# All eight row groups of the up pairs in a 7-product form, more low parts by accumulating DMA, and new order tables

## The chip, the cores and the metric

The kernel runs on one core of a Trainium2 chip. The metric is the device time of one execution in microseconds: the median of the runs that were taken. Lower is better.

## The reference

One inference step of a hybrid diffusion backbone with one trunk layer, for 128 context tokens and 128 latent tokens (both request groups use the same weights, so 256 rows go through every weight matrix):

```python
D_MODEL = 2048; D_FF = 4 * D_MODEL; IN_WIDTH = 8704
sh1, sc1, g1, sh2, sc2, g2 = ada_mod(c_ctx, w_ada, b_ada)       # SiLU(c) @ w_ada + b_ada
h = rms_norm(xp, norm1_w) * (1 + sc1) + sh1
qa, ka, va, qb, kb, vb, ga, gb = project_heads(h, w_in, ...)
oa = context_attention(qa, ka, va, sink)                        # latent: window / neighbourhood attention
ob = context_attention(qb, kb, vb, None)
xp = xp + g1 * merge_branches(oa, ob, ga, gb, w_br_a, w_br_b, w_out)
h2 = rms_norm(xp, norm2_w) * (1 + sc2) + sh2
xp = xp + g2 * sq_relu_mlp(h2, w_up, w_down)                    # relu(h2 @ w_up) ** 2 @ w_down
```

All is float32. The outputs are both groups' tokens and the new keys and values.

## The kernel before

**Products.** Each float32 operand is split in a high part (a rounded copy, by ScalarE) and a low part (the operand less its high part), and a product is three matmuls: high by high, high by low, low by high. A matmul takes a 128x128 stationary operand (128 rows of the contracted dimension, 128 tokens) and 512 moving columns of a weight.

**Steps.** The weights stream through in 456 steps, one 128x1024 float32 tile (0.524 MB) each. `add_step` records a step, `run` (L284 on) emits all of them in one order for all engines, ahead of the run; nothing is scheduled by the machine except that each engine and queue runs its own list in order and waits on semaphores. Per step the raw tile is loaded on SP's queue, ScalarE makes `wH` (`prep_hi`), VectorE makes `wL` (`prep_b`), TensorE multiplies. Steps 0 to 71 are the first input projections, 72 to 135 the gates, 136 to 167 the branches, 168 to 199 `w_out`, 200 to 215 up units 0 and 1. Then come seven periods of 32 steps: an up pair p (units 2p and 2p+1 of 512 columns of `w_up`, 16 steps) and the four down units of pair p-1 (4 steps each); at last four down units (440 to 455).

**Tables that set the order.** `RUN[i]` says how many steps ahead of step i raw tiles are requested, `LOOK[i]` how many steps ahead high and low parts are made; high parts go one step further (`HI_AHEAD`). `LO_DMA` lists the steps whose low part is made by DMA: ScalarE writes the negated high part (`minus_plus`, L265), then a DMA issued by GpSimd (POOL's queue) adds the raw weight to it from HBM (L266). `DOTS`, `DOTS2`, `POST`, `JOBS` and others place side work (dot products for the modulation, attention, transposes of activations) at steps.

**Buffers.** Nearly all tiles come from one pool, `G`, of GEN = 50 general buffers of 4 KB per partition. A load waits until the buffer it takes is free.

**Up pairs.** In `up_pair` a row group is 256 rows of the contracted dimension: two halves k, two token groups s and the two units n make a 2x2 by 2x2 block product, 8 products. Six of the eight row groups (0, 2, 3, 5, 6, 7) are done with 7 products on sums of blocks, into seven PSUM banks Q1 to Q7: the weights come rearranged (`in_w_upF`) as tiles X and Y, `y_sums` and `y_split` make the sums t and u with their high and low parts on VectorE and ScalarE, and `fast_stat` prepares the sums of the stationary side once (`sH`, `sL`, for three of the four groups of h2). Row groups 1 and 4 are plain: two weight tiles, 8 products, some of them into an eighth bank Z, which VectorE adds at the end. After a pair, `up_act` (relu, square), `up_planes`, `up_flip` (a DMA transpose on SP's queue), `up_T` and `up_T_lo` turn its output into stationary operands `aH`, `aL` for the down units.

**Down units.** Down unit n of piece p adds to a running sum of 512 output columns; for n = 1, 2, 3 the sum is copied out of PSUM, stored to HBM by POOL (`sm`), loaded back on SP (`sum_back`) and seeded into PSUM by ScalarE. Gates in `AWAY` are stored and loaded back in the same way.

## Time and profile before

| what | value |
|---|---|
| runs | 1316.84, 1318.39, 1317.2 us; median 1317.2 |
| span of the profiled execution | 1317.5 us |
| its mean granted TensorE clock | 0.998 |
| one period (up pair and four down units) | 83.0 us |
| low parts by accumulating DMA | 33 (21 of them in the seven periods) |
| DMA, whole span | 417.98 MB, mean 317 GB/s |

The profiled execution's own time is its span, 1317.5 us, since what lies around it is not part of the page; it stands 0.3 us from the median. The page lists busy time by engine, where PE is TensorE's matmul, PEld its weight load, DVE VectorE, ACT ScalarE, POOL GpSimd and SP SyncE. A busy share is a mean over stages with different limits, so the stages are looked at one by one.

### The profile page before, as it was taken

The numbers are of one execution on the slowest core, as the hardware profiler recorded it, in microseconds if no ns is written. First come the engines' busy times: TensorE is split into PE (matmuls) and PEld (weight loads), VectorE is DVE, ScalarE is ACT, GpSimd is POOL, SyncE is SP. The second block draws the span as 40 slices with busy tenths as digits, with TensorE's granted clock in tenths as the row PEclk, the third lists the DMA queues.
The fourth block names the chain that finished last, engine by engine and source line by source line (L and its number), as shares of the span: only waits on it lengthen the run. The fifth ranks groups of instructions, "written<-read, shape, count | busy, mean of one in ns | idle before, by whom it ended". The sixth has DMA issues, their size and how long they took to land.

```text
span 1317.5 us, 18232 instructions
## 1 busy us (share of the span) xinstructions
PE 1304.1 (99%) x6320; PEld 1061.0 (81%) x6320; DVE 1149.2 (87%) x1490; ACT 915.0 (69%) x1282; POOL 78.3 (6%) x99
## 2 busy tenths in 40 slices
PE   8999999999999999999999999999999999999998
PEld 4777788788888878888888888888888888888876
DVE  4478899985999989999899799897988988979996
ACT  5534766788766555654788868969779688796772
POOL 0000003211000000000000000100101001010010
PEclk9999999999999999999999999999999999999999
DMA  9999999987699999997489878989989799899994
GB/s 371 408 408 409 408 335 358 370 304 285 210 367 340 371 371 330 340 388 267 163 264 324 271 256 292 291 295 296 323 293 291 265 313 305 286 287 370 351 345 168
DMA packets 154972, 417.98 MB, mean 317 GB/s; under 512 B 52688, under 2 KB 53952, under 8 KB 154880
## 3 DMA queue, kind: packets, MB, share of 16 engines
q1 hardware_dynamic: 146128, 386.54, 79.9%
q0 software_dynamic: 8560, 30.18, 9.9%
q8 instruction: 49, 0.80, 0.3%
q14 instruction: 43, 0.35, 0.1%
q10 hardware_dynamic: 192, 0.10, 0.1%
HBM read 389.19 MB, written 17.61 MB: 309 GB/s over the span
## 4 chain that ended last, share of the span: by engine, by line
PE 97%; DMA 2%; ACT 0%; DVE 0%; issue 0%
PE acc L312 17%; PE acc L314 17%; PE acc L313 17%; PE Q L1211 7%; PE Q L1213 7%; PE Q L1212 6%; PE acc L423 5%; PE acc L424 5%; PE acc L425 5%; DMA araw<-in_w_pair 2%; PE ps_ada L329 2%; PE ps_S L775 1%; PE acc L1028 1%; PE acc L1046 1%; PE acc L1029 1%; PE acc L1044 1%
## 5 line engine op out<-in xcount | busy, mean ns | idle before, releaser
L101 ACT ACTIVATE wH<-raw 128x1024 fp32r<-128x1024 f32 (+1 forms) x375 | 378.3, 1045 | 122.8 <-DMA raw<-in_w_in 19.7
L259 DVE TENSOR_TENSOR wL<-raw,wH 128x1024 fp32r<-128x1024 f32 x336 | 399.7, 1223 | 50.8 <-ACT wH L101 28.1
L423 PE MATMUL acc<-wH,hH 128*128 128x512 f32 x276 | 108.8, 394 | 0.0
L425 PE MATMUL acc<-wH,hL 128*128 128x512 f32 x276 | 107.6, 390 | 0.0
L424 PE MATMUL acc<-wL,hH 128*128 128x512 f32 x276 | 107.6, 390 | 0.0
L312 PE MATMUL acc<-wH,hH 128*128 128x512 f32 x256 | 102.4, 400 | 0.0
L314 PE MATMUL acc<-wH,hL 128*128 128x512 f32 x256 | 99.9, 390 | 0.0
L313 PE MATMUL acc<-wL,hH 128*128 128x512 f32 x256 | 99.8, 390 | 0.0
L1422 DVE CUSTOM_DVE_ANT_0 aT<-aT,cB,cols 128x1024 f32<-128x1024 f32 x60 | 76.4, 1289 | 0.1
L1422 DVE CUSTOM_DVE_ANT_0 junk<-aT,cB,cols 128x1024 bf16<-128x1024 f32 x60 | 76.4, 1290 | 0.0
L423 PEld LDWEIGHTS acc<-wH,hH 128*128 128x128 f32 x276 | 51.8, 188 | 12.9 <-issue 2.1
L101 ACT ACTIVATE uH<-raw 128x1024 fp32r<-128x1024 f32 x42 | 44.4, 1057 | 24.0 <-DVE raw L1270 22.9
L425 PEld LDWEIGHTS acc<-wH,hL 128*128 128x128 f32 x276 | 51.8, 188 | 11.0
L424 PEld LDWEIGHTS acc<-wL,hH 128*128 128x128 f32 x276 | 51.9, 188 | 10.3
L1276 DVE TENSOR_TENSOR tL<-t,tH 128x1024 fp32r<-128x1024 f32 x42 | 51.3, 1221 | 8.6 <-ACT tH L101 8.6
L101 ACT ACTIVATE tH<-t 128x1024 fp32r<-128x1024 f32 x42 | 44.3, 1056 | 20.6 <-DVE t L1266 15.0
L312 PEld LDWEIGHTS acc<-wH,hH 128*128 128x128 f32 x256 | 48.1, 188 | 10.1 <-issue 0.7
L314 PEld LDWEIGHTS acc<-wH,hL 128*128 128x128 f32 x256 | 48.1, 188 | 10.2
L313 PEld LDWEIGHTS acc<-wL,hH 128*128 128x128 f32 x256 | 48.2, 188 | 9.8 <-issue 0.5
L1266 DVE TENSOR_TENSOR t<-raw 128x1024 f32<-128x1024 f32 x42 | 51.2, 1220 | 1.8 <-PE acc L314 1.4
L1258 DVE TENSOR_TENSOR XL<-raw,XH 128x1024 fp32r<-128x1024 f32 x42 | 51.2, 1220 | 0.4 <-DMA sm<-dsum 0.4
L1276 DVE TENSOR_TENSOR uL<-raw,uH 128x1024 fp32r<-128x1024 f32 x42 | 51.2, 1219 | 0.0
(626 smaller groups left out, 3387.8 us busy)
## 6 DMA issues: line engine op xcount, KB each, us to landing
raw<-in_w_in SPq DMA_DIRECT2D x133, 512.0 KB, 9.4
raw<-in_w_down SPq DMA_DIRECT2D x128, 512.0 KB, 6.5
raw<-in_w_upF SPq DMA_DIRECT2D x84, 512.0 KB, 5.6
araw<-in_w_pair SPq DMA_DIRECT2D x72, 512.0 KB, 10.2
aT<-in_w_gT SPq DMA_DIRECT2D x64, 512.0 KB, 8.5
aT<-in_w_adaT SPq DMA_DIRECT2D x56, 512.0 KB, 9.0
raw<-in_w_up SPq DMA_DIRECT2D x44, 512.0 KB, 6.3
raw<-in_w_out SPq DMA_DIRECT2D x32, 512.0 KB, 10.4
```

The costliest lines, as they stand in the source:

```text
L101: act.activation(out, in_, AF.Copy)
L259: dve.tensor_tensor(st["lo"], st["raw"], st["hi"].bitcast(F32), op=OP.subtract)
L312: pe.matmul(acc[tb], sh, wh[:, k, :], start=f, stop=False, **kw)
L313: pe.matmul(acc[tb], sh, wl[:, k, :], start=False, stop=False, **kw)
L314: pe.matmul(acc[tb], sl, wh[:, k, :], start=False, stop=l, **kw)
L423: pe.matmul(acc[tb], sh, wh[:, k, :], start=kt == 0 and k == 0 and not held and not seeded, stop=False, **kw)
L424: pe.matmul(acc[tb], sh, wl[:, k, :], start=False, stop=False, **kw)
L425: pe.matmul(acc[tb], sl, wh[:, k, :], start=False, stop=last and k == 1 and not hold, **kw)
L1211: pe.matmul(acc, stat[0], hi, start=f, stop=False)
L1213: pe.matmul(acc, stat[1], hi, start=False, stop=l)
L1276: dve.tensor_tensor(b[n + "L"], v, b[n + "H"].bitcast(F32), op=OP.subtract)
L1422: dve.tensor_tensor_reduce(out, box["raw"], cB[s, tag], 1.0, dst if second else baT[:, part, fb:fb + 1], OP.mult, OP.add, dst)
```

## The change

Row groups 1 and 4 of the seven pairs take the 7-product form too. The stationary sums of the fourth group of h2 (`fast_stat(3)`) find no buffers of their own: they are written over halves of `h2H`/`h2L` that only up units 0 and 1 read, after up unit 1. Bank Z and its additions fall away. `LO_DMA` grows from 33 to 86 steps and may now hold X tiles (`x_lo_dma`); the low parts of `a2` and `a3` come the same way (`TL_DMA`). Where X's low part is still made by VectorE, it moves into `y_sums` (`XLO_IN`). Four of the running sums stay in their buffers (`STAY`), four gates instead of five go away and back. GEN is 54: the descriptor scratch of GpSimd's DMAs shrinks to 2048, a small pool of scratch tiles is replaced by general buffers. Joins of transposed halves, relu, square and the copies around them are placed one by one (`U_AT`), the lead of high parts has a table of its own (`HIA`), and all order tables are new. The new functions `qk_planes`, `qk_flip`, `qk_join` and `probs_planes` are not called, since `POST` and `JOBS` give three and five places.

```diff
-GEN = 50
+GEN = 54
-FAST = {1: (0, 2, 3, 5, 6, 7), ...}
+FAST = {1: (0, 1, 2, 3, 4, 5, 6, 7), ...}
-AWAY = [('gB', 2), ('gA', 0), ('gB', 0), ('gA', 2), ('gB', 3)]
+AWAY = [('gB', 0), ('gB', 3), ('gA', 1), ('gB', 1)]
-HI_AHEAD = 1
+HIA = "000012322005501123521100232312000100221230331146547320002112220001012200000001..."
-LO_DMA = [57, 92, 106, 114, 116, 127, 165, 172, 184, 196, 224, 232, 237, 256, ...]
+LO_DMA = [45, 47, 51, 67, 83, 84, 85, 91, 92, 94, 98, 100, 110, 112, 116, 118, ...]
+XLO_IN = True
+STAY = [(3, 1), (3, 2), (5, 2), (5, 3)]
+TL_DMA = [2, 3]
...
 def lo_dma(st):
+    if "lo_dma" in st:
+        st.pop("lo_dma")(st)
+        return
...
+            def x_lo_dma(st, b=b):
+                if "prep_a" in st:
+                    st.pop("prep_a")()
+                b["XL"] = G("XL", F32R)
+                minus_plus(b["XL"], b["XH"], st["src"])
...
+        if g == 3:
+            for q in range(nfast - 6):
+                for i in range(2):
+                    dst = [x[2 * q + i].rearrange("p (c k) s t -> p c k s t", k=2)[:, :, 0, 1, :] for x in (h2H, h2L)]
+                    split(*dst, t[:, 2 * i:2 * i + 2, q, :])
+            return
...
         def sc(j, c):
+            if j > 5:
+                g, k = 2 * (j - 6) + c // 2, 2 * (c % 2)
+                return h2H[g][:, k, 1, :], h2L[g][:, k, 1, :]
             return sH[j // 2][:, c, j % 2, :], sL[j // 2][:, c, j % 2, :]
...
-        if seeded and p < last:
+        if seeded and p < last and (p - 1, n) not in STAY:
             load_at(len(wsteps) - SUM_BACK, lambda: sum_back(p, n))
...
-            if n in SEED_N and p < last - 1:
+            if n in SEED_N and p < last - 1 and (p, n) not in STAY:
...
+            for n, places in zip(PIECES[p + 1], U_AT[p]):
+                fs = (lambda n=n: up_act(n, AF.Relu), lambda n=n: up_act(n, AF.Square), lambda n=n: up_planes(n, (0,)),
+                      lambda n=n: up_planes(n, (1,)), lambda n=n: up_flip(n), lambda n=n: join_half(("a", n), 0),
+                      lambda n=n: join_half(("a", n), 1), lambda n=n: up_hi(n), lambda n=n: up_T_lo(n))
...
-    nc = bacc.Bacc("TRN2", target_bir_lowering=False, num_devices=1)
+    nc = bacc.Bacc("TRN2", target_bir_lowering=False, num_devices=1, dynamic_dma_scratch_size=2048)
```

What this does to TensorE's list, in pair 1. Before, the first six matmuls of plain row group 1, whose first tile goes into Q2 and Q4 (two such sets of six per tile, two tiles):

```order
L1211 MATMUL Q2_6518<-wH_6371,h23H_6028 128x512
L1212 MATMUL Q2_6518<-wL_6401,h23H_6028 128x512
L1213 MATMUL Q2_6518<-wH_6371,h23L_6029 128x512
L1211 MATMUL Q4_6535<-wH_6371,h23H_6028 128x512
L1212 MATMUL Q4_6535<-wL_6401,h23H_6028 128x512
L1213 MATMUL Q4_6535<-wH_6371,h23L_6029 128x512
```

Now every row group has products of X, YB, t and u; these are the first twelve matmuls of the seventh, with stationary sums out of `h20H` and `h21H`:

```order
L1295 MATMUL Q1_6535<-XH_6709,h23H_6064 128x512
L1296 MATMUL Q1_6535<-XL_6725,h23H_6064 128x512
L1297 MATMUL Q1_6535<-XH_6709,h23L_6065 128x512
L1295 MATMUL Q3_6579<-XH_6709,h21H_6034 128x512
L1296 MATMUL Q3_6579<-XL_6725,h21H_6034 128x512
L1297 MATMUL Q3_6579<-XH_6709,h21L_6035 128x512
L1295 MATMUL Q2_6537<-YB_6729,h23H_6064 128x512
L1296 MATMUL Q2_6537<-YB_6729,h23H_6064 128x512
L1297 MATMUL Q2_6537<-YB_6729,h23L_6065 128x512
L1295 MATMUL Q5_6581<-tH_6796,h20H_6023 128x512
L1296 MATMUL Q5_6581<-tL_6797,h20H_6023 128x512
L1297 MATMUL Q5_6581<-tH_6796,h20L_6024 128x512
```

The 24 matmuls of a plain row group have become 21; over the program TensorE's list is 42 matmuls of 128x512 shorter.

VectorE's list before, at the start of pair 2: the first row group (t13 and the halves of raw are the sums, XL, tL, uL low parts), then the two low parts of plain row group 1:

```order
L1266 TENSOR_TENSOR t13_7102<-raw_6983,raw_7002 128x1024
L1268 TENSOR_TENSOR raw_7002<-t13_7102,raw_6983 128x512
L1269 TENSOR_TENSOR YB_7103<-raw_7002,YB_7103 128x512
L1270 TENSOR_TENSOR raw_7002<-raw_7002 128x512
L1258 TENSOR_TENSOR XL_7109<-raw_6983,XH_7078 128x1024
L1276 TENSOR_TENSOR tL_7128<-t13_7102,tH_7127 128x1024
L1276 TENSOR_TENSOR uL_7132<-raw_7002,uH_7131 128x1024
L259 TENSOR_TENSOR wL_7158<-raw_7055,wH_7125 128x1024
L259 TENSOR_TENSOR wL_7176<-raw_7057,wH_7156 128x1024
```

The same place now:

```order
L1361 TENSOR_TENSOR t13_7100<-raw_7060,raw_7062 128x1024
L1363 TENSOR_TENSOR YB_7101<-raw_7062,YB_7101 128x512
L1364 TENSOR_TENSOR raw_7062<-t13_7100,raw_7060 128x512
L1367 TENSOR_TENSOR raw_7062<-raw_7062 128x512
L1361 TENSOR_TENSOR t13_7198<-raw_7064,raw_7082 128x1024
L1363 TENSOR_TENSOR YB_7199<-raw_7082,YB_7199 128x512
L1364 TENSOR_TENSOR raw_7082<-t13_7198,raw_7064 128x512
L1367 TENSOR_TENSOR raw_7082<-raw_7082 128x512
L1373 TENSOR_TENSOR tL_7206<-t13_7100,tH_7205 128x1024
L1373 TENSOR_TENSOR uL_7210<-raw_7062,uH_7209 128x1024
```

XL has left for the DMA queue here, the second row group has its own sums in place of two low parts, and its sums stand ahead of the first one's splits.

GpSimd's list before, from pair 1 to pair 2 (`sm` are sums stored away):

```order
L266 DMA wL_6504<-in_w_up 128x1024
L266 DMA wL_6726<-in_w_down 128x1024
L266 DMA wL_6844<-in_w_down 128x1024
L1353 DMA sm01_7053<-dsum1_7050 128x1024
L1353 DMA sm02_7152<-dsum2_7149 128x1024
L1353 DMA sm03_7216<-dsum3_7213 128x1024
```

And now, the last transfers of pair 1, its down units and the start of pair 2:

```order
L272 DMA XL_6725<-in_w_upF 128x1024
L272 DMA XL_6774<-in_w_upF 128x1024
L272 DMA wL_6987<-in_w_down 128x1024
L272 DMA XL_7086<-in_w_upF 128x1024
L272 DMA XL_7097<-in_w_upF 128x1024
L1452 DMA sm01_7126<-dsum1_7123 128x1024
L1452 DMA sm02_7196<-dsum2_7193 128x1024
L272 DMA XL_7248<-in_w_upF 128x1024
L1452 DMA sm03_7283<-dsum3_7280 128x1024
L272 DMA XL_7285<-in_w_upF 128x1024
```

All eight low parts of X in pair 1 come by this queue; the sums now stand between accumulating transfers. Over the program POOL issues 88 of those instead of 33, 50 of them in the seven periods.

204 lines of the change are left out of this document (135 added, 69 removed).

## The prediction

> **What bounds the kernel now.** I read the page first: its busy table and the chain that ended last.
>
> ```profile
> span 1317.5 us, 18232 instructions
> PE 1304.1 (99%) x6320; PEld 1061.0 (81%) x6320; DVE 1149.2 (87%) x1490; ACT 915.0 (69%) x1282; POOL 78.3 (6%) x99
> PE 97%; DMA 2%; ACT 0%; DVE 0%; issue 0%
> ```
>
> TensorE has work in 99% of the span, and 97% of the chain is its own work: at almost every step the instruction before it on PE is what held it. But a matmul's end is modelled, so I looked next at the table by stage. I cut it at the first matmul of each stage; 683.3 is the start of up pair 1, and each later row up to 1181.3 is one period (an up pair, then the four down units of the pair before). Columns: length, then busy time and count of PE, PEld, DVE, ACT and POOL, granted clock, DMA share, GB/s.
>
> ```profile
> 456.60:548.00 91.40, 91.40 (x454) 74.45 (x453) 85.41 (x115) 56.03 (x55) 1.72 (x2) 1.00 1.01 347
> 683.30:766.20 82.90, 82.90 (x367) 68.70 (x366) 71.62 (x81) 67.91 (x72) 3.74 (x5) 1.00 0.87 279
> 766.20:849.20 83.00, 83.00 (x368) 68.73 (x367) 76.37 (x86) 66.20 (x73) 4.25 (x6) 1.00 0.86 287
> 849.20:932.10 82.90, 82.90 (x367) 68.70 (x366) 73.52 (x82) 65.95 (x73) 4.26 (x6) 1.00 0.91 287
> 932.10:1015.10 83.00, 83.00 (x367) 68.74 (x367) 73.83 (x82) 66.62 (x74) 5.13 (x7) 1.00 0.91 306
> 1015.10:1098.10 83.00, 83.00 (x368) 68.75 (x367) 72.54 (x82) 64.98 (x72) 4.30 (x6) 1.00 0.88 291
> 1098.10:1181.30 83.20, 83.20 (x369) 68.77 (x368) 75.53 (x84) 66.59 (x76) 5.35 (x8) 1.00 0.91 303
> 1181.30:1267.00 85.70, 83.37 (x367) 68.38 (x366) 81.64 (x98) 63.30 (x70) 4.53 (x7) 1.00 1.01 353
> 1267.00:1317.50 50.50, 45.60 (x194) 37.13 (x194) 40.23 (x58) 18.16 (x24) 5.04 (x8) 0.94 0.66 227
> ```
>
> By the program a period holds 174 matmuls of an up pair (58 products of three) and 192 of the down units, all of 128x512, so 366 in 83.0 us: **0.2268 us each**, at the full granted clock (1.00), the same in every period. The periods have no PE idle time at all, so each matmul taken out there is time taken out. The one place where PE waits late in the program is the end of the seventh period (83.37 of 85.70). The chain in order of time (start, us, what) shows it:
>
> ```profile
> 1264.49 1.06 ACT dsum L101 x2
> 1265.61 0.78 issue
> 1266.38 0.61 ACT acc L101
> ```
>
> There PE waits some 2.7 us for banks that ACT first has to empty and seed.
>
> **What is removed.** A plain row group costs 2 weight tiles x 2 k x 2 token groups = 8 products, the 7-product form 7. Two row groups in seven pairs change, each product being three matmuls: 2 x 7 x 3 = 42 matmuls x 0.2268 = **-9.5 us**, all on the path. The stationary operands stay as many per product, so the rate should not change. From the profile's own 1317.5 (the runs' median is 1317.2, so the two agree within 0.3) this gives 1308.0.
>
> **What it adds to VectorE and ScalarE.**
>
> ```profile
> L259 DVE TENSOR_TENSOR wL<-raw,wH 128x1024 fp32r<-128x1024 f32 x336 | 399.7, 1223 | 50.8 <-ACT wH L101 28.1 <-PE acc L313 9.4 <-issue 8.1
> L1276 DVE TENSOR_TENSOR tL<-t,tH 128x1024 fp32r<-128x1024 f32 x42 | 51.3, 1221 | 8.6 <-ACT tH L101 8.6
> L1266 DVE TENSOR_TENSOR t<-raw 128x1024 f32<-128x1024 f32 x42 | 51.2, 1220 | 1.8 <-PE acc L314 1.4 <-PE acc L313 0.5
> L1258 DVE TENSOR_TENSOR XL<-raw,XH 128x1024 fp32r<-128x1024 f32 x42 | 51.2, 1220 | 0.4 <-DMA sm<-dsum 0.4
> L1268 DVE TENSOR_TENSOR raw<-t,raw 128x512 f32<-128x512 f32 x42 | 29.1, 692 | 1.4
> L1269 DVE TENSOR_TENSOR YB<-raw,YB 128x512 fp32r<-128x512 f32 x42 | 28.8, 685 | 2.0 <-ACT YB L101 2.0
> L1311 DVE TENSOR_TENSOR up<-up,Z 128x512 f32<-128x512 f32 x7 | 4.8, 688 | 0.2
> L1422 DVE CUSTOM_DVE_ANT_0 aT<-aT,cB,gc_g 128x1024 f32<-128x1024 f32 x32 | 40.6, 1282 | 0.1
> L101 ACT ACTIVATE tH<-t 128x1024 fp32r<-128x1024 f32 x42 | 44.3, 1056 | 20.6 <-DVE t L1266 15.0 <-PE Q L1213 2.1 <-PE Z L1213 1.6
> L101 ACT ACTIVATE XH<-raw 128x1024 fp32r<-128x1024 f32 x42 | 44.2, 1052 | 8.5 <-PE Q L1212 4.6 <-DMA raw<-in_w_upF 2.2 <-PE Q L1213 1.2
> L265 ACT ACTIVATE wL<-wH 128x1024 fp32r<-128x1024 f32 x33 | 35.1, 1063 | 1.1
> L101 ACT ACTIVATE YB<-raw 128x512 fp32r<-128x512 f32 x42 | 25.9, 618 | 3.7 <-PE Z L1213 2.8 <-PE acc L313 0.8 <-PE Q L1212 0.2
> ```
>
> A row group in the new form costs DVE t, tL, uL, XL (4 x 1.22), two sums of half width (2 x 0.692) and YB (0.685): 6.95 us. The plain one cost two low parts, 2.45. For 14 groups: +63.0; the seven additions of Z go, -4.8. Against this stand the low parts taken off DVE. In the stretch of the seven periods 21 of them came by DMA, and now 50 do (48 of weights, two of activations): 29 x 1.22 = -35.4. In all **DVE +22.8 us** there. Its busy time there is the sum of the seven rows, 525.1 of 583.7; now it is 548 of the 574.2 that PE needs, 95% where it was 90%. ACT gets XH, YB, tH, uH for two wH (3.78 for 2.1), 14 times, +23.5, and 29 negated copies of 1.063, +30.8: 461.6 becomes 516, 90%. Both engines still fit below PE; that is the cover, and with 26 us of DVE room over seven periods it is thin. If it were gone, each further us on DVE would be a us of span.
>
> Over the rest of the program 26 more low parts leave DVE (26 x 1.22 = 32 us) and come to ACT and the DMA queues; DVE gains room there, and I cost it at nothing.
>
> **The last stretch.** In the seventh period DVE had 81.64 busy of 85.70, since dot products for the last gate stand there. There the two groups add 13.9 to DVE, plain low parts by DVE (two) go, -2.45, two more low parts come by DMA, -2.4, Z goes, -0.7, and two dot jobs of two 1.28 us each move out to the next unit, -5.1: +3.2, so 84.8 of work for 84.3 us (85.7 less 1.36). I take **+2 us** for it, between -2.7 (the wait at 1264 vanishes) and +5 (the dots gain nothing by moving).
>
> **What it adds to the DMA engines.**
>
> ```profile
> q1 hardware_dynamic: 4481, 16.32, 102.3%
> ...
> q0 software_dynamic: 215, 0.82, 105.4%
> ...
> q0 software_dynamic: 713, 2.62, 54.2%
> q1 hardware_dynamic: 1021, 3.71, 47.6%
> ...
> q1 hardware_dynamic: 146128, 386.54, 79.9%
> q0 software_dynamic: 8560, 30.18, 9.9%
> ...
> pTa<-pla SPq DMA_TRANSPOSE x16, 5.2
> ```
>
> The first row is a stretch of 40 us (100 to 140) with plain loads alone, full at a share of 102%: 0.524 MB in 40 x 0.524 / 16.32 = 1.284 us. The second is 4 us (1091 to 1095) with only POOL's queue, full as well: 4 x 0.524 / 0.82 = **2.56 us for one accumulating transfer**, two loads' worth. From the whole page it comes dearer: q0's 9.9% are 130.4 us for 57.6 units of 0.524 MB, of which 33 accumulate; the others at q1's mean (79.9% for 738 units, 1.43 us) leave 95.2 / 33 = 2.9 us. So 2.56 to 2.9.
>
> Is there room? I count the stretch of seven periods by the order of the queues: 224 weight loads, 36 sums out and back, 29 loads for dots, 12 for conditions and x1, at 1.284 = 387; 15 transposes at 3.2 (my estimate, half way between one load and the 5.2 us to landing), 48; 21 accumulating at 2.56, 54: 489 of 583.7. Afterwards there are 29 more, and eight sum transfers fewer: 489 + 74 - 10 = 553 of 574. The third and fourth rows (843 to 863, full at 102%) test such a count: 3.71 MB of q1, three accumulating transfers and two sums of q0 make 9.1 + 7.7 + 2.6 = 19.4 of 20 us, 3% short. With this 3% the engines need 570 of 574: **nearly a tie with PE**. At 2.9 it is 588, and PE would run dry. I take 2.56, the row in which the queue was alone, and cost the tie at nothing: at 456.60 the engines stood at 1.01 for 91 us and PE did not wait.
>
> ```profile
> HBM read 389.19 MB, written 17.61 MB: 309 GB/s over the span
> ```
>
> The Trainium skill (Perfetto Trace Analysis, Identifying the Most-Contended Engine) would judge this otherwise: DMA by the use of HBM's bandwidth, not by occupancy, which 16 engines make misleading. By that rule 309 GB/s, against the 409 that 16.32 MB in 40 us are, leave a quarter free, and the DMA rival below falls away. This trace differs: from 843 to 863 the engines are full while (2.62 + 3.71) / 20 us is 317 GB/s, because accumulating transfers cost twice their bytes. I keep the rival.
>
> **Smaller edits, each nothing.** XL is computed among y's sums instead of ahead of them, on the same engine. `fast_stat` of group 3 waits for the end of up unit 1, whose matmuls read the halves it overwrites; queued behind its copies on ACT are pair 1's first XH. Its data are wanted 12 steps on, 28 us later; if ACT's lead is lost, a us or two. Split joins, relu and square in pieces, and scratch in general buffers change who waits in the shadow of PE. STAY and one gate fewer spare ten transfers. More prepared in POOL's queue means sums queue behind low parts there, and POOL is busy 6%.
>
> **Rivals.**
> 1. *The DMA engines become the bound*, in the seven periods. At 2.9 us the excess is 588 - 574 = 14 us: 1308 + 14 = **1322** (1315 to 1330), slower. It decides from about 2.64 us per accumulating transfer on, where the count passes 574. For it: the tie, and seven periods without a slack one. Against: a stretch at 1.01 with no PE wait. The Trainium skill (Trainium Kernel Development and Optimization, Key Constraints) has the ground of it: transfers of SP, ACT and POOL share the same 16 DMA engines, so a second queue brings no second bandwidth.
> 2. *VectorE becomes the bound*, at the up pairs, where all of t, u and YB are needed. In the second one it has no room even now, and lives on what it prepared before:
>
> ```profile
> 766.20:805.70 39.50, 39.50 (x176) 32.70 (x175) 39.12 (x43) 26.01 (x29) 1.42 (x2) 1.00 0.82 284
> ```
>
> If a period loses 1 us to it, seven take back 7: **1315**, the same as before. For: 95% over the stretch. Against: the period from 1181 ran at 95% (81.64) and lost 2.3.
> 3. *PE runs without any wait*: 1308.0 - 2.7 = **1305**. That needs the end wait gone, though DVE there gets fuller.
>
> That the change would not do what it says can be set aside: the order on PE has the 42 matmuls fewer.
>
> **How the numbers follow.** Forecast: 1308.0 + 2 = **1310**, own range 1306 to 1314, chance 0.63. Rival 1: 0.17, rival 2: 0.14, rival 3: 0.06. Faster by over 0.2% (which is about what a measurement of this kernel can tell from no change) means below 1314.6, slower above 1319.8: faster 0.63 + 0.06 + 0.05 of rival 2 = 0.74; the rest of rival 2 and a little of rival 1, 0.11, are the same; slower 0.15. The range 1305 to 1321 leaves out most of rival 1 and the lower half of rival 3.
>
> **What would show it.** Right: a period of 81.6 us with PE busy throughout, DMA share about 1.0, DVE about 77 and ACT about 74 of it, and a wait of a few us around the last period's end. Rival 1: PE or ACT waiting for `raw`, `wL` or `XL` transfers at a share of 1.02. Rival 2: PE waiting for `tL`, `uL` or `wL` of DVE with the DMA share below 1. What would make it wrong most easily is the order: prepared less far ahead in many places, a late low part meets PE at once.

## The result, and the profile after

The changed kernel takes **1347.66 us** (median of 4 runs, 1345.13 to 1353.53) against 1317.02 us for before (1316.61 to 1318.39): ratio 1.0233, interval 1.021 to 1.0257. It is 30 us slower, where 1310 was forecast, and outside the range given. The profiled execution has a span of 1345.3 us; its run took 1347.07, so what lies around a span is some 1.8 us. It is 1.8 us for before too (in the runs beside e1 a time of 1316.76 us has a span of 1315.0). So the profiled execution of before, span 1317.5, was a run of some 1319.3 us by this estimate, 2 us above its median and not 0.3, and the forecast took a span for a time. All comparisons by stage below are of span with span.

First the page of the changed kernel: its span, the busy table, and the chain that ended last by engine.

```profile
span 1345.3 us, 18444 instructions
PE 1306.6 (97%) x6278; PEld 1055.0 (78%) x6278; DVE 1142.5 (85%) x1506; ACT 984.1 (73%) x1388; POOL 125.0 (9%) x150
PE 60%; DMA 21%; issue 9%; DVE 6%; ACT 2%; POOL 0%; SPq 0%; ACTq 0%; DVEq 0%; POOLq 0%
```

The 42 matmuls are gone (6278 for 6320), and VectorE is busy 7 us less than before. But the chain, 97% TensorE's own before, is now 60% that and 21% DMA. The table by stage (same columns as in the prediction; `...` stands for a row left out; from 688.10 on each row is one period; the last row is the four down units of the last pair and the end, called the last unit below):

```profile
455.70:548.20 92.50, 92.09 (x454) 74.32 (x453) 84.00 (x113) 53.50 (x55) 1.73 (x2) 1.00 1.05 361
548.20:628.30 80.10, 77.79 (x345) 63.66 (x344) 74.64 (x99) 48.12 (x57) 6.78 (x8) 1.00 1.01 359
...
688.10:785.30 97.20, 86.68 (x362) 70.64 (x361) 74.29 (x90) 72.37 (x85) 8.10 (x10) 0.95 1.03 268
785.30:871.00 85.70, 82.17 (x361) 67.40 (x360) 78.41 (x90) 73.83 (x85) 7.76 (x10) 1.00 0.99 315
871.00:954.00 83.00, 82.34 (x362) 67.36 (x362) 77.38 (x88) 69.88 (x81) 7.77 (x10) 1.00 0.97 314
954.00:1036.80 82.80, 82.36 (x362) 67.32 (x360) 75.21 (x86) 69.84 (x82) 6.63 (x8) 1.00 0.94 299
1036.80:1118.90 82.10, 81.93 (x362) 67.53 (x361) 75.51 (x86) 71.15 (x82) 9.52 (x12) 1.00 1.01 311
1118.90:1210.00 91.10, 85.48 (x363) 68.83 (x362) 79.78 (x90) 75.65 (x89) 6.55 (x9) 0.96 0.90 286
1210.00:1291.90 81.90, 81.90 (x361) 67.45 (x361) 78.72 (x96) 66.28 (x76) 5.75 (x8) 1.00 1.01 343
1291.90:1345.30 53.40, 44.87 (x195) 35.64 (x193) 40.81 (x57) 22.23 (x28) 6.87 (x10) 1.00 0.81 273
```

A period without waits should take 360 matmuls at 0.2268 us, 81.6 us. The fifth and the seventh do. The loss is lumped: **15.6 us in the first period, 9.5 in the sixth, 4.1 in the second**, and outside the periods some 3 us each in the output stage (80.1 us; 77.05 before) and in the last unit (53.4; 50.5 before). The seven periods together take 603.8 us, 29.6 more than the prediction's 574.2.

The first period's loss lies in its up pair (53.65 us; the rest of the period takes the 43.5 us of 192 matmuls). The waits of 700 to 736 us (us in total, times, longest), and the one piece of the chain there that is not TensorE's:

```profile
DVE uL L1373 <- DMA pTa<-pla: 11.9, 1, 11.9
PE Q L1296 <- DMA XL<-in_w_upF: 5.3, 1, 5.3
PE Q L1296 <- DVE uL L1373: 5.2, 1, 5.2
```
```profile
701.17 31.68 DMA pTa<-pla
```

So TensorE waits twice in it: 5.3 us for a low part of X that comes by accumulating transfer (issued at 702.45, landed 15.1 us later; the median of these is 8.7), and 5.2 us for a low part of u, before which VectorE stood 11.9 us until a DMA transpose had landed. That low part does not read what the transpose writes; by the code, both take their buffers from the pool `G`, and it waits for one that the transpose still holds. The transpose, of up unit 1's output, took **31.7 us to land**; before, the median was 5.2. The timeline of SP's queue and that of POOL's (start, length of the issue) show what it met:

```profile
701.17 14.23 SPq L953 DMA_TRANSPOSE pTa<-pla  x1
715.49 7.13 SPq L231 DMA_DIRECT2D raw<-in_w_down  x2
```
```profile
702.45 0.87 POOL L272 DMA_DIRECT2D XL<-in_w_upF  x1 [5.34 <-ACT XL L271]
706.76 0.87 POOL L272 DMA_DIRECT2D XL<-in_w_upF  x1 [3.45 <-DMA cB<-silu]
712.21 0.87 POOL L272 DMA_DIRECT2D XL<-in_w_upF  x1 [4.58 <-ACT XL L271]
```

SP was held 14.2 us by the issue of that transpose alone; the next weights left only at 715.5, though TensorE lost nothing by that in this period. On POOL's queue three accumulating transfers ran beside it. The transpose's first packet ran 9.3 us after its issue began, its last 20.2 us after that. The DMA queues in the 20.2 us in which the transpose's packets ran (its 2048 packets have 256 bytes), and in the 2.4 us of a nearly undisturbed transpose of the same kernel:

```profile
DMA packets 2425, 1.75 MB, mean 87 GB/s; under 512 B 2125, under 2 KB 2125, under 8 KB 2425
q1 hardware_dynamic: 2144, 0.75, 68.5%
q0 software_dynamic: 281, 1.01, 54.5%
...
XL<-in_w_upF POOLq DMA_DIRECT2D x1, 512.0 KB, 21.1
pTa<-pla SPq DMA_TRANSPOSE x1, 31.7
```
```profile
DMA packets 2093, 0.68 MB, mean 283 GB/s; under 512 B 2055, under 2 KB 2055, under 8 KB 2093
q1 hardware_dynamic: 2077, 0.61, 112.9%
q0 software_dynamic: 16, 0.07, 13.6%
```

The engines count as full in both, but move 87 GB/s in the first. Counted from the trace, a transpose's packet took 89 ns there on average and 19 to 37 ns in the other 18 transposes of the kernel; 246 of POOL's packets of 4 KB began inside it. In before all 19 transposes ran 1.8 to 4.4 us, and only one of them had more than one such packet inside (21). So the working theory after the result: **collisions**, a transpose and accumulating transfers that slow each other, with what hangs on either of them: TensorE's low part, VectorE's buffer, and at other places the weights' plain loads behind the transpose in SP's order. The rivals: **volume** (too many bytes for the transfer engines over a whole period, the prediction's rival 1), **VectorE** (its rival 2), and **order** (the new tables issue things late whoever makes the low parts).

A second thing makes each stall dearer. The two gaps and what follows each, in the columns of the table by stage (the third number from the end is the granted clock):

```profile
711.95:717.63 5.68, 0.39 (x3) 0.01 (x1) 4.52 (x6) 2.31 (x3) 0.87 (x1) 0.94 0.88 58
717.63:719.60 1.97, 1.97 (x5) 1.59 (x6) 0.00 (x0) 0.00 (x0) 0.00 (x0) 0.50 1.16 83
728.60:734.22 5.62, 0.39 (x3) 0.00 (x1) 1.28 (x2) 0.00 (x0) 0.00 (x0) 0.99 0.90 246
734.30:736.50 2.20, 2.20 (x5) 1.73 (x6) 2.20 (x3) 0.00 (x0) 0.00 (x0) 0.50 1.03 412
```

After a gap of 5.7 us the clock is **0.50**; by the trace's clock record it stays there 6.8 us after the first and 3.4 us after the second. TensorE idles 5.29 and 5.23 us in them (length less the busy 0.39), and the half clock costs (6.8 + 3.4) / 2 = 5.1: together 15.6, the loss of the period.

### The profile page after: what moved, and what is told of

Same layout as the page of the kernel before. It is cut to its first block, busy times and chain, and to the rows that moved or that the text cites. A ratio compares the mean times of both kernels' runs of the same rounds, so it can differ in the third digit from the quotient of the medians.

```text
span 1345.3 us, 18444 instructions
## 1 busy us (share of the span) xinstructions
PE 1306.6 (97%) x6278; PEld 1055.0 (78%) x6278; DVE 1142.5 (85%) x1506; ACT 984.1 (73%) x1388; POOL 125.0 (9%) x150
## 4 chain that ended last, share of the span: by engine, by line
PE 60%; DMA 21%; issue 9%; DVE 6%; ACT 2%; POOL 0%; SPq 0%; ACTq 0%; DVEq 0%; POOLq 0%
PE acc L323 9%; PE acc L324 9%; PE acc L325 9%; PE acc L434 5%; PE acc L436 4%; PE acc L435 4%; PE Q L1296 4%; PE Q L1295 4%; PE Q L1297 4%; DMA pTa<-pla 4%; DMA raw<-in_w_br_b 3%; DMA raw<-in_w_out 3%; DMA araw<-in_w_pair 2%; DMA raw<-in_w_in 2%; DMA raw<-in_w_up 2%
## 5 line engine op out<-in xcount | busy, mean ns | idle before, releaser
L103 ACT ACTIVATE wH<-raw 128x1024 fp32r<-128x1024 f32 (+1 forms) x347 | 348.4, 1043 | 131.1 <-DMA raw<-in_w_in 28.7
L265 DVE TENSOR_TENSOR wL<-raw,wH 128x1024 fp32r<-128x1024 f32 x283 | 334.1, 1223 | 40.3 <-ACT wH L103 27.8
L1522 DVE CUSTOM_DVE_ANT_0 junk<-aT,cB,cols 128x1024 uint8<-128x1024 f32 x60 | 77.4, 1291 | 4.6 <-DMA aT<-in_w_gT 3.8
L1373 DVE TENSOR_TENSOR uL<-raw,uH 128x1024 fp32r<-128x1024 f32 x56 | 68.3, 1220 | 15.2 <-DMA pTa<-pla 11.9
L1361 DVE TENSOR_TENSOR t<-raw 128x1024 f32<-128x1024 f32 x56 | 68.3, 1220 | 11.7 <-DMA raw<-in_w_upF 6.5
L1373 DVE TENSOR_TENSOR tL<-t,tH 128x1024 fp32r<-128x1024 f32 x56 | 68.3, 1220 | 9.9 <-ACT tH L103 6.6
L103 ACT ACTIVATE XH<-raw 128x1024 fp32r<-128x1024 f32 x56 | 58.8, 1050 | 20.9 <-DMA raw<-in_w_upF 14.8
L271 ACT ACTIVATE wL<-wH 128x1024 fp32r<-128x1024 f32 x58 | 61.1, 1059 | 5.7 <-PE acc L324 4.3
L103 ACT ACTIVATE tH<-t 128x1024 fp32r<-128x1024 f32 x56 | 58.7, 1048 | 4.8 <-DVE t L1361 3.2
L436 PEld LDWEIGHTS acc<-wH,hL 128*128 128x128 f32 x276 | 51.8, 188 | 10.9
## 6 DMA issues: line engine op xcount, KB each, us to landing
raw<-in_w_in SPq DMA_DIRECT2D x133, 512.0 KB, 10.2
araw<-in_w_pair SPq DMA_DIRECT2D x72, 512.0 KB, 10.2
aT<-in_w_adaT SPq DMA_DIRECT2D x56, 512.0 KB, 10.2
```

Of the source, the lines that this page charges most:

```text
L103: act.activation(out, in_, AF.Copy)
L265: dve.tensor_tensor(st["lo"], st["raw"], st["hi"].bitcast(F32), op=OP.subtract)
L271: act.activation(lo, hi.bitcast(F32), AF.Copy, scale=-1.0)
L436: pe.matmul(acc[tb], sl, wh[:, k, :], start=False, stop=last and k == 1 and not hold, **kw)
L1361: dve.tensor_tensor(t.rearrange("p (a n) -> p a n", a=2), X.rearrange("p (a n) -> p a n", a=2), Y[:, 0:512].unsqueeze(1).to_broadcast([P, ...
L1373: dve.tensor_tensor(b[n + "L"], v, b[n + "H"].bitcast(F32), op=OP.subtract)
```

## The experiments

Times are medians; each ratio is to before's runs on the same chip. "Span" is that of the profiled execution.

**e1: the transpose of unit 1 seven steps earlier**, so that it comes before the accumulating transfers of pair 1.

```diff
-P_UP = [1, 8]
+P_UP = [1, 1]
```

> One number: the planes and the DMA transpose of up unit 1's output are issued 7 steps earlier (P_UP[1] 8 to 1), which by the profile of the changed kernel falls between 692 and 700 us, where POOL's queue moves nothing. Collision theory (a DMA transpose that meets accumulating transfers takes 20 us instead of 3 and holds up SP's queue behind it): up pair 1 falls from 53.6 us to 38 to 41, the run from 1347.7 to about 1333. Volume theory (the engines have too much to move in this period, 11 accumulating transfers): pair 1 stays above 48, the run within 4 us of 1347.7. Order theory (VectorE and ScalarE make X, t and u too late): no change beyond 3 us.

Measured: 1335.5 us (1.0124, 1.0093 to 1.0154), span 1334.5. Pair 1 alone, in after and here:

```profile
688.15:741.80 53.65, 43.13 (x170) 34.60 (x169) 37.99 (x47) 35.27 (x43) 3.46 (x4) 0.90 1.10 258
```
```profile
686.33:725.10 38.77, 38.49 (x169) 31.37 (x168) 36.54 (x45) 34.91 (x43) 3.46 (x4) 1.00 1.04 315
```

The stall is gone, with the same 4 accumulating transfers issued in the pair and the engines again over 1.0. A DMA share of 1.04 by itself costs TensorE nothing: only 0.3 us of 38.8 are lost. The transpose, now with none of POOL's packets beside it, ran 3.1 us. This is the collision theory's prediction at this place, and it moves 12 of the 30 us. The rest stays elsewhere: 5.6 us at 770, 6.4 at 1181, 5.1 at 1291.

**e2: unit 1's output transposed by TensorE** instead of by DMA.

```diff
-        at(end_of(("up", n)) + P_UP[n], lambda: up_planes(n))
+        if n == 1: at(end_of(("up", n)) + P_UP[n], up_pe); return
+        at(end_of(("up", n)) + P_UP[n], lambda: up_planes(n))
```

(`up_pe` makes eight 128x128 transposes into PSUM and the high and low parts from there.)

> Unit 1's output is transposed by TensorE (8 transposes, 0.9 us by the 0.11 us each that others take) in place of the DMA transpose; all accumulating transfers stay. Collision theory: pair 1 at 39 to 42 us, the run about 1333. Volume theory: only 0.5 MB fewer of some 28 MB in the period, the run above 1343. Order theory: no change, or slower by the transposes' 0.9 us.

Measured: 1337.18 us (1.0142, 1.0127 to 1.0158), span 1335.1. Pair 1 takes 46.1 us, more than the collision theory's 39 to 42: the two long gaps are gone, but ScalarE now waited 10.0 us and VectorE 7.1 us in their own order for that transpose on TensorE, and their sums for the pair came late. So for the pair it exchanges one in-order wait for another. That the total agrees with e1 is luck: the first period is 7.3 us longer here (89.6 for 82.3) and the sixth 9.7 us shorter (83.9 for 93.6), though nothing was edited there.

**e3: the eight low parts of X in pair 1 by VectorE** instead of by accumulating DMA.

```diff
-LO_DMA = [..., 216, 218, 220, 222, 224, 226, 228, 230, 242, ...]
+LO_DMA = [..., 242, ...]
```

> The eight low parts of X in pair 1 are made by VectorE instead of by accumulating DMA; the DMA transpose stays where it is. Collision theory and volume theory both say that pair 1's stall goes (38 to 43 us, the run 1331 to 1337); the transpose in the trace is then back at about 3 us. Order theory: VectorE gets 8 x 1.2 = 10 us more in this period, pair 1 stays at 50 or more, the run at 1345 to 1355.

Measured: 1336.49 us (1.0128, 1.0106 to 1.015), span 1339.4. Pair 1:

```profile
688.60:733.30 44.70, 39.56 (x169) 31.08 (x168) 44.48 (x53) 31.55 (x39) 0.00 (x0) 1.00 0.73 256
```

Without accumulating transfers the transfer engines have room (0.73) and the stall is gone: unit 1's transpose, at its place of after, ran 3.3 us in place of 20.2. So either partner taken away, the transpose in e1 or the transfers here, ends the collision. But VectorE is busy 44.48 of 44.70: rival 2, at home inside an up pair. A pair in the new form cannot have all its low parts on VectorE; that is what the accumulating transfers were for.

**e5: row groups 1 and 4 plain again**, with everything else of after.

```diff
-FAST = {1: (0, 1, 2, 3, 4, 5, 6, 7), ...}
+FAST = {1: (0, 2, 3, 5, 6, 7), ...}
```

> Everything of the change but the two row groups: six in the 7-product form, groups 1 and 4 plain again, with the 86 accumulating transfers and the new tables. 42 matmuls more (+9.5 us). Collision and volume theory: the stalls stay where they are, the run is 1347.7 + 9.5 - up to 6 us for VectorE's relief: 1350 to 1358. Order theory (the new form is what overloads VectorE and ScalarE): the stalls go, the run is 1316 to 1325.

Measured: 1335.64 us (1.0123, 1.0096 to 1.015), span 1332.6. It lies between the expectations and meets neither: the tables and the accumulating transfers alone cost 18 us over before, and the 7-product form, which takes 9.5 us off TensorE, comes out 12 us dearer on top. The same collision is there in both (unit 1's transpose ran 7.9 us here, 20.2 in after), and pair 1 takes 44.2 and 53.7 us; why it is shorter here is open.

**e4 and e8: the accumulating transfers below step 216 put back to before's ten**, alone and together with e1's edit; **e7: before, with after's 33 there instead**.

```diff
-LO_DMA = [45, 47, 51, 67, ..., 204, 207, 215, 216, ...]
+LO_DMA = [57, 92, 106, 114, 116, 127, 165, 172, 184, 196, 216, ...]
```

(e8 has `P_UP = [1, 1]` too; in e7 the 33 numbers stand ahead of before's own from 224 on, and a raw tile that is not there yet is requested at once.)

> After, with the accumulating transfers of the steps below 216 (attention, gates, branches, output projection) put back to the ten that before has, 23 fewer, and VectorE forming those 23 low parts. The 41 steps from 216 on are as in after. Load theory (the queue of accumulating transfers makes the weight loads of the branch and output stages late): the 3.1 us of the output stage, 1.0 us of the branch stage and 1.4 us of the third output unit go, output stage 77 us instead of 80.2, time about 1342. Order theory (the new tables issue those loads late, whoever makes the low parts): output stage stays at 80 us, time 1346 to 1349.

> The run before this one and the earlier transpose of unit 1's output (e1_flip_early, 1335.5 us) together. If the two losses are separate and both come from the accumulating transfers, 1330; if the output stage's loss is the order's, 1335; if what is saved ahead comes back as a later stall in the pairs, again 1335 but with an output stage of 77 us and a longer stall behind it.

> Before, with its own tables and six groups, but with the 33 accumulating transfers that after has below step 216 in place of its ten; from step 216 on before's own. Load theory: the output stage goes from 77 to 80 us and the time to about 1322. Order theory: nothing changes, 1317, or, VectorE having 23 sums less, up to 2 us less.

Measured: e4 1375.8 us (1.0436, 1.0397 to 1.0476), e8 1360.72 (1.0327, 1.0296 to 1.0358), e7 1346.11 (1.0202, 1.0178 to 1.0227). All three miss, in both directions: fewer transfers made after slower by 28 us, more of them made before slower by 29. In e4 the loss is in the attention part (first two stages 226.2 and 220.1 us for 214.5 and 211.0), and its largest single wait there is

```profile
PE acc L435 <- DMA wL<-in_w_in: 9.1, 1, 9.1
```

a low part whose transfer stands on POOL's queue behind attention's small operations. A list of accumulating transfers is worth something here only with the order it was made for, and these three say little on the load as such. One thing they do say: e4 and e8 lie 15 us apart, as after and e1 do (12), so e1's gain is local. In e4 unit 1's transpose again ran 19.8 us beside 246 of POOL's packets, in e8 4.1 us beside 11.

**e6: 23 steps in `LO_DMA` instead of 86.**

```diff
-LO_DMA = [45, ..., 216, 218, 220, ..., 452]
+LO_DMA = [57, 92, 106, 114, 116, 127, 165, 172, 184, 196, 224, 232, 237, 282, 288, 329, 352, 378, 384, 416, 436, 448, 449]
```

> After with 23 accumulating transfers instead of 86 (those of before, without the ten whose place in the pairs no longer exists), VectorE forming the other 63 low parts. Theory of the accumulating transfers: the stalls at 712 and 729 us, the half clock behind them and the stalls of the second pair and of the unit of 1192 us go; what is left is VectorE's sums, of which the seven periods get 40 more (about 1.06 us each, 42 us): VectorE would then have some 587 us of work in 566 us of matmuls, so the loss moves to VectorE, 1325 to 1332. Order theory (queue places and buffers, not the transfers): the same stalls stay and VectorE comes on top, 1355 to 1370.

Measured: 1381.51 us (1.0477, 1.0458 to 1.0497), span 1376.6: above both expectations. The first stages lose what e4 loses; in the periods the fifth, for one, shows VectorE at 87.1 of 88.7 us and the transfer engines at 0.79:

```profile
1059.35:1148.02 88.67, 84.22 (x361) 68.23 (x360) 87.11 (x98) 66.54 (x77) 3.38 (x5) 0.98 0.79 265
```

So the forecast's rival 2 is real, and the accumulating transfers do hold it off. (The expectation took 1.06 us for a low part; VectorE needs 1.22.)

**e9: e1, and local edits at its remaining stalls**: unit 3's transpose two steps later, six accumulating transfers at the places of its stalls back to VectorE.

```diff
-U_AT = [[[...], [8, 8, 11, 12, 12, 19, 19, 19, 20]], ...
+U_AT = [[[...], [8, 8, 11, 12, 14, 19, 19, 19, 20]], ...
-LO_DMA (of e1)
+LO_DMA (of e1 without 175, 374, 384, 404, 407, 441)
```

> e1_flip_early (1335.5 us) with local edits at the places of its remaining stalls: the transpose of unit 3 two steps later, past the store of the sums beside which it took 6.6 us, and the six accumulating transfers of steps 175, 374, 384, 404, 407 and 441 back to VectorE (six sums of 1.22 us more). Collision theory (each stall is a transpose, and the plain loads queued behind it on SP, held up by accumulating or storing packets at that place): the losses at 770 (5.6 us), 1181 (6.4), 1106 and 1132 to 1144 (5.2), 570 (1.2) and 1291 (5.1) go for the most part, time 1316 to 1322. Volume theory (too many bytes for the transfer engines over each period): six transfers of 86 change little, the stalls move to other places, 1330 to 1336.

Measured: **1321.78 us** (1.0027, 1.0013 to 1.0042), span 1317.9. 80 transfers instead of 86 and two transposes moved take back 26 of the 30 us, as the collision theory said; how much each of the edits carries is not separated. What happens at one place, in the down units of the sixth period: after's SP, POOL and ScalarE first.

```profile
1181.28 4.49 SPq L953 DMA_TRANSPOSE pTa<-pla  x1
1185.86 4.49 SPq L231 DMA_DIRECT2D raw<-in_w_upF  x5
```
```profile
1178.66 0.86 POOL L272 DMA_DIRECT2D wL<-in_w_down  x1 [9.01 <-ACT wL L271]
1184.60 0.56 POOL L1452 DMA_DIRECT2D sm<-dsum  x1 [5.08 <-ACT dsum L103]
1185.67 0.87 POOL L272 DMA_DIRECT2D wL<-in_w_down  x1 [0.51 <-ACT wL L271]
```
```profile
1193.65 1.06 ACT L103 ACTIVATE XH<-raw 128x1024 fp32r<-128x1024 f32 x1 [8.33 <-DMA raw<-in_w_upF]
```

And the same step of e9, without the two transfers of `wL`:

```profile
1159.20 2.88 SPq L953 DMA_TRANSPOSE pTa<-pla  x1
1162.17 14.12 SPq L231 DMA_DIRECT2D raw<-in_w_upF  x6
```
```profile
1166.17 1.06 ACT L103 ACTIVATE XH<-raw 128x1024 fp32r<-128x1024 f32 x1 [2.08 <-DMA raw<-in_w_upF]
```

In after the first raw tile behind the transpose reaches ScalarE 7.8 us after its issue, ScalarE stands 8.3 us with the copies for the sums queued behind, and TensorE waits 4 us; in e9 it is 4.0 us and 2.1 us, and TensorE does not wait. The same place is without a stall in e2 and e8 too (sixth period 83.9 and 84.9 us), with both transfers of `wL` in the list, so the list alone does not make the stall: it hangs on what comes together at that moment.

**e10: e1 without the 32 loads of the second gate's weights**; the second gate's values are then not the reference's, VectorE's work stays.

```diff
     def dot_load(box, job, h):
+        if which == "g2":
+            return
```

> e1_flip_early (1335.5 us) without the 32 loads of the second gate's weights (16.8 MB of plain loads, all from step 230 on); VectorE makes the same products from another tile, so its work stays, and the second gate holds the wrong values. Volume theory: 32 x 1.28 us = 41 us of transfer work leaves the seven periods, the stalls there go, stages from the first pair on as before the change or better, 1315 to 1320. Collision theory: the transposes at 762 and 1172 us still meet stores and accumulating packets; the stalls at 770 and 1181 us stay, only those where loads land late (1106, 1291) shrink, 1326 to 1332. VectorE theory: nothing changes, 1335.

Measured: 1320.3 us (1.0011, 1.0001 to 1.0021), span 1319.2. So 16.8 MB less plain load does as much as e9's few places. The time is at the edge of the volume theory's range and well below the collision theory's. Two stalls stay: the second pair loses 3.8 us (6.1 in e1), with unit 3's transpose still 4.5 us beside 128 of POOL's packets, and the sixth 4.6 (5.3 in e1). That at 1181 goes with the loads, and the last unit comes to 48.7 us, under before's 50.5. So less load cures it too, and outside the first period the runs do not decide between collision and volume. My reading, which both runs fit but neither shows, is that a full set of engines has nothing left to make good the moment in which a transpose holds SP; either less load or a transpose elsewhere restores that.

**e12 to e15: what is left, tried from both sides.** All are e9 without the accumulating transfer of step 262, and with these edits (`M_AT` places the branch result's copies, transpose and join):

```diff
 # e12
-U_AT[6] = [[1, 7, 8, 9, 9, 12, 12, 12, 14], [7, 10, 10, 10, 11, 14, 14, 14, 14]]
+U_AT[6] = [[1, 4, 5, 6, 6, 9, 9, 9, 11], [5, 7, 7, 7, 8, 11, 11, 11, 12]]
-M_AT = [2, 4, 8]
+M_AT = [2, 4, 9]
 # e13
+LO_DMA: 441 again
-DOTS2 = [..., 422, 423, 427, 432, 432, 432, 432, 433, 438, 438, 440, 443, 443, 444, 444, 444]
+DOTS2 = [..., 424, 424, 426, 426, 428, 431, 431, 432, 436, 437, 439, 439, 440, 443, 444, 444]
 # e14
+DOTS2 = [..., 422, 423, 427, 432, 432, 432, 432, 433, 434, 435, 436, 441, 442, 443, 444, 444]
+M_AT = [1, 3, 8]
 # e15
+U_AT[6] = [[1, 7, 8, 9, 9, 12, 12, 12, 14], [7, 10, 10, 10, 11, 15, 15, 15, 15]]
+M_AT = [2, 3, 8]
```

> e9_clear (1321.8 us, profiled span 1317.9) with three further local edits: the accumulating transfer of step 262 (11.2 us to land, for which PE waited at 802 us) back to VectorE; the copies, transposes and joins of the last two units' outputs three steps earlier (VectorE stood 4.3 us at 1262 us for the joined planes of unit 15, with the low parts that PE wanted at 1266 behind it); and the third low part of the branches' result one step later (VectorE stood 3.8 us at 556 us for it, with nine low parts behind). If each wait is what its place in the engine's order makes it, the losses at 560 (1.4 us), 802 (2.1) and 1266 (5.1) go and the span comes to 1309 to 1311, time 1311 to 1314. If VectorE or the transfers are simply full at these places, the same time is lost some steps later, 1318 to 1323.

> e9_clear with step 262 back to VectorE and, for the last unit, another cure: the last 16 loads and products of the second gate at the steps of before (spread, where after has four at one step), and the accumulating transfer of step 441 in again. If the crowd of eight gate products (10 us of VectorE) and loads makes the last unit late, its 54.9 us come down to about 50.5 as before and the time to 1314 to 1317; if the place of the last unit's transpose and join makes it, the last unit stays at 53 to 55 us and the time at 1319 to 1322.

> e9_clear (profiled span 1317.9 us, last unit 54.9) without the transfer of step 262, and with two local edits: five of the last loads and products of the second gate one to four steps earlier (ahead of the two transposes of the last pair's outputs, behind which the transfer engines are full of plain loads from 1260 to 1274 us), and the transposes of the branches' result one step earlier (SP stood 9.2 us at one of them with the output weights' loads behind it). Load theory for what is left: the last unit comes down from 54.9 to 49 to 51 us, the output stage from 79.0 to 77 to 78, span 1310 to 1313. Order theory (the joins' and sums' places on ScalarE and VectorE): the last unit stays at 53 to 55 us, span 1315 to 1318.

> The same base with the rival's edits: the join of unit 15's planes one step later (ScalarE reached it at 1263.4 us, 5 us after its transpose had ended, and VectorE stood 4.3 us for it with the low parts that PE wanted at 1266 behind), the gate's loads where they were; and of the branches' transposes only the flip one step earlier. Order theory: the last unit 50 to 52 us, span 1312 to 1315. Load theory: last unit unchanged at 54 to 55 us, span 1315 to 1318.

Measured: 1330.01 us (1.0093, 1.008 to 1.0106), 1327.83 (1.0068, 1.0055 to 1.0081), 1320.54 (1.002, 1.001 to 1.0029), 1323.71 (1.0042, 1.0027 to 1.0056). Step 262's transfer was a real stall: the second pair takes 38.1 to 38.2 us in all four, 40.2 in e9. The other edits missed: in e12 the output stage is 8 us longer than in e9 (87.0 for 79.0), and in each of them the last two units together (the last unit and the four down units before it) were longer than e9's 98.6 us (e12 102.5, e13 107.1, e14 100.5, e15 101.2). Neither "load" nor "order" explains that stretch alone.

**e16 and e17: e9 without step 262's transfer and with step 441's again**; in e17 raw tiles of steps 160 to 172 may also start up to two steps earlier.

```diff
-LO_DMA (of e9)
+LO_DMA (of e9 without 262, with 441)
 # e17
-RUN[160:173] = "6886154244868"
+RUN[160:173] = "8998376466989"
```

> e9_clear (1321.8 us, profiled span 1317.9) without the transfer of step 262 and with that of step 441 as after has it. By the stages seen so far the second pair takes 38.1 us (40.2), the last two units together 97 to 98 us as in after and e1_flip_early (98.6 in e9_clear), the rest as in e9_clear: span 1314 to 1316, time 1315 to 1319. If the transfer of step 441 meets the last two transposes, the last two units take over 99 us and the time is 1320 to 1324.

> The run before this one, with the plain loads of steps 160 to 172 (up to the output stage's start) allowed to start two steps earlier. If the loss at 560 us (1.4 us) is one of late weight loads (ScalarE waited for raw weights at 556 and 558 us, ahead of the high part that VectorE's nine low parts stood behind), output and branch stages shrink by 1 to 2 us, time 1314 to 1317; if the loads are held by their buffers or by a transpose, nothing changes there.

Measured: **1318.9 us** (1.0004, 0.9996 to 1.0013) and 1319.84 (1.0009, 0.9997 to 1.0021): no difference from before that can be measured. e17's profiled execution (span 1314.4; a run of 1316.21 us, near the low end of its runs, 1315.59 to 1323.4) shows what the change can do. Its first and its seventh period, then the sum of its seven, then that of after:

```profile
685.44:767.72 82.28, 82.21 (x361) 67.39 (x360) 74.73 (x91) 74.88 (x87) 8.10 (x10) 1.00 1.04 313
...
1179.15:1260.78 81.63, 81.63 (x361) 67.56 (x360) 80.22 (x99) 65.30 (x75) 5.76 (x8) 1.00 1.03 344
sum 575.34, PE 573.98 PEld 472.16 DVE 543.59 ACT 493.78 POOL 47.79; mean PE 82.00 PEld 67.45 DVE 77.66 ACT 70.54 POOL 6.83
```
```profile
sum 603.76, PE 582.81 PEld 476.53 DVE 539.25 ACT 498.95 POOL 52.08; mean PE 83.26 PEld 68.08 DVE 77.03 ACT 71.28 POOL 7.44
```

575.3 us for the seven periods, 1.1 over the prediction's 574.2, and 8.4 under before's 583.7, with engines at 1.03 and 1.04 and no wait worth naming. Not all of the 8.4 is matmuls: 2.3 of it is the wait that ended before's seventh period, and a wait of 3.0 us now stands in the last unit behind. The gain is given away in the branches (93.6 us for 91.5), the output stage (78.3 for 77.1) and the last unit (53.7 for 50.5). In e16 the last unit's wait is SP's:

```profile
1261.90 4.89 SPq L1509 DMA_DIRECT2D aT<-in_w_gT  x3
1267.53 3.72 SPq L231 DMA_DIRECT2D raw<-in_w_down  x3
```

Three gate loads hold SP, the longest time for the landing of an earlier weight (3.0 us), which by my reading frees their buffer; the weights behind them take 11.0 us to land, and TensorE waits 3.4 us at 1277.

**e18: e17 with unit 6's transpose two steps earlier; e19: that, with five of the last six gate products one to three steps later** (`ROW_AT` keeps the row that uses the last of them at its step).

```diff
 # e18
-U_AT[2][0] = [-1, -1, 11, 12, 12, 13, 14, 14, 14]
+U_AT[2][0] = [-1, -1, 9, 10, 10, 13, 14, 14, 14]
 # e19, besides
-DOTS2 = [..., 438, 438, 440, 443, 443, 444, 444, 444]
+DOTS2 = [..., 438, 438, 441, 443, 444, 445, 446, 447]
-ROW_AT = [5, 7, 9, 5]
+ROW_AT = [5, 7, 9, 2]
```

> e17_run (1319.84 us; profiled span 1314.4) with the transpose of unit 6 two steps earlier. In the two runs before, PE waited 0.9 us and 3.4 us (half clock behind it) at 934 us for ScalarE, which joined that unit's planes late. If the distance between transpose and join is what varies there from execution to execution, the wait goes, and the times come closer together: median 1316 to 1318.5; if it is the transfers around it, 1319 to 1321.

> The run before this one with the last six products of the second gate up to three steps later, so that SP issues their loads between the last weights' loads and not ahead of them (three of them held SP 4.9 us for buffers at 1262 us, with the weights behind them on the queue, and PE waited 3.8 us at 1276 for the weights). If the last unit's loss is that place on SP's queue, it comes from 54 us to 49.5 to 51, and the time to 1311 to 1314, under both kernels; if the transfer engines' volume there makes it, whatever the order, the last unit stays at 53 to 54 us and the time at 1317 to 1320; if VectorE's products come too late for the last gate row, the loss moves to the last 10 us.

Measured: 1319.46 us (1.0011, 1.0002 to 1.002) and 1328.86 (1.0084, 1.0071 to 1.0098). e18 changes nothing that these runs can tell. In e19 the loads do go between the weights, but the gate's last products are then late: TensorE waits 9.5 us at 1294 for the column that they make. That is the third outcome named, so whether place or volume holds the last unit is **not settled**; only that without those loads (e10) it takes 48.7 us. No kernel of this study beats before.

## Why the prediction was wrong, step by step

- **What bounds the kernel, and the price of a matmul: right.** Periods without waits take 81.6 to 82.1 us, as said; -9.5 us is in TensorE's work. e17's periods are 8.4 us shorter, 2.3 of it the end wait that went elsewhere.
- **VectorE's sum: right, a little high.** Forecast 548 us in the seven periods, measured 539; ScalarE 516 forecast, 499 measured. The cover held; e3 and e6 show how near rival 2 was.
- **The failed step is the tie.** The prediction counted the transfer engines at 570 of 574 us, took 2.56 us per accumulating transfer, "the row in which the queue was alone", and "cost the tie at nothing: at 456.60 the engines stood at 1.01 for 91 us and PE did not wait". Two things were wrong in it.
  - *The size.* By the prediction's own rows, share times length summed over before's seven periods is 530 us, not the 489 that the count by queues gave; the 3% was tested on one stretch of 20 us. In after the sum is 591, in e17 560 of 575. These sums count too much: 1.55 in the 5.9 us ahead of the first gap shows that packets overlap on an engine, so time in which one waits for another counts as well. The two queues over after's seven periods show the price of an accumulating transfer:

```profile
q1 hardware_dynamic: 70122, 149.62, 70.6%
q0 software_dynamic: 9295, 33.49, 27.1%
```

  POOL's 33.49 MB are 64 units of 0.524 MB, 47 of them accumulating; the other 17 at q1's mean (70.6% of 603.8 us for 285.5 units, 1.49 us) leave (163.6 - 25.3) / 47 = 2.9 us. That is the dearer of the two prices, which the mean over the whole of before had already given, and it too holds what the packets wait in a crowd.
  - *What matters more, the kind of thing.* A share is not what makes TensorE wait: pair 1 at 1.04 loses 0.3 us in e1, and the row at 456.60 was such a place too. What makes it wait is a moment: a transpose among accumulating packets, each slowed by the other, with TensorE's next operand, or the buffer for it, behind one of them. In pair 1 that is shown: with the transpose moved (e1) or the transfers gone (e3), it runs 3.1 and 3.3 us for 20.2, and 14.9 and 9.0 us of the pair come back. For the sixth period and the rest it is argued from e9, and e10 leaves volume open there. The 456.60 stretch had hardly any of that. The prediction counted 15 transposes at 3.2 us as load and never asked what stood beside each on the other queue, or behind it on its own; the order of POOL's list was in the text, and the step of moving unit 1's transpose into eight accumulating transfers (P_UP from 3 to 8) was not looked at.
- **Rival 1 was the right resource and the wrong shape.** It spread 14 us evenly (1322, to 1330). The loss came in lumps, 15.6 and 9.5 us in two of seven periods, a third or more of it (5.1 of 15.6) by what follows a gap: half clock. Its sign of recognition, waits for `raw` and `XL` at a share of 1.03, is what the profile shows.
- **The last stretch: wrong place.** The seventh period runs without a wait (81.90 of 81.90; before it lost 2.3, where the prediction took 2.7), so the +2 on 84.3 us is -2.4 there, the low end of the range given; the last unit behind it, which got no term, costs 2.9 us.
- **What lies outside the periods, costed at nothing: wrong by about 5 us,** most of it in the output stage (3.1) and the stages beside it; e17's earlier loads take 0.7 us off that stage (to e16) and add 0.9 to the branches ahead of it, and e7 shows that another list below step 216 can cost 29.
- **"Prepared less far ahead in many places, a late low part meets PE at once"** was named as what would most easily make it wrong. It did so at 802 us in e9 (step 262's XL, 11.2 us to land) and in the output stage, for some 2 us each. The larger stalls were a late XL beside a transpose, that transpose, and late raw weights.

The sum of the miss: 603.8 - 574.2 = 29.6 us in the periods, 7.7 us around them, together the 37.3 between 1308.0 and 1345.3.

The prediction set aside the Trainium skill's rule on DMA (Perfetto Trace Analysis, Identifying the Most-Contended Engine), HBM use instead of occupancy, for the occupancy. The runs side with neither measure as a verdict: 268 GB/s and a share of 1.03 stand in the worst period, 313 GB/s and 1.04 in the same period of e17 without a stall. The Trainium skill (DMA: Bandwidth & Descriptors, Queues, rings and completion order) says that each engine goes round-robin between the queues it has work for, a whole packet at a time, a packet being there some 9 to 17 descriptors. Whether the profile's packets of 256 bytes are such packets no run here shows. Turns that are waited for would look like 89 ns instead of 19 to 37, and POOL's 4-KB packets took 0.72 us in that stretch too, 0.25 us beside the transpose at 1183; but no run here separates this from a slowdown inside the transpose.

## What to carry to other kernels

Before adding transfers on a second queue, list for every DMA transpose what runs beside it on the other queue, what stands behind it on its own, and who waits for its buffers: the share of the engines over a period does not show this, and moving one transpose by seven steps was worth 12 us here. Tables that place such transfers are fitted to each other; a list taken over into another order, in either direction, cost 28 us. A forecast of "full but not over" should price the first stall too, with the clock that is lost behind it.

## What the runs showed of the hardware that was not expected

- A DMA transpose of 0.52 MB ran 1.8 to 5.0 us where at most five of POOL's 4-KB packets began beside it, in all kernels here. Beside 49 to 132 it ran 3.0 to 9.2 us, and in pair 1 of after and of e4, beside 246, 20.2 and 19.8 us. The count of packets alone doesn't set the time: in pair 1 of e5 it was 7.9 us beside some 110, in the third period of e14 3.4 us beside 119.
- While it ran for 20.2 us, the engines counted as full at 87 GB/s. The two queues' shares there add up to 123%, so occupancy counts time in which packets wait for each other as well.
- After every gap of TensorE of 3.4 us or more, in all kernels here, the granted clock was 0.50 for 3.4, 6.8 or 10.2 us. Of 23 gaps of 2.3 to 3.4 us, 18 were followed by it, four were not, and one lay in such a stretch already. Below that it followed three single gaps of 1.9 to 2.0 us, and else only series of shorter ones. In the 3.4 us just before each drop TensorE had idled 1.5 us or more. A matmul then takes twice its 0.23 us (0.43 in the chain at 735), so each us of it costs half a us of work. The Trainium skill (TensorE: Matmul & The Clock Gate, The HAM clock gate) states a free-running window of some 3.4 us for this; the trace agrees, in multiples of 3.4. Idle time well short of such a window was enough here, though; the measurement decides.
- Kernels near the edge spread more: e9's ten runs go from 1318.4 to 1327.8 us, before's nineteen on the same chip from 1316.9 to 1320.8. The one profile of such a kernel can lie nearly 4 us from its median, as e17's does.
